# Three modulation sections of layer 0 moved from the Hyena and SSD stretch to the filters at the start

## The chip, the core and the metric

The kernel runs on one NeuronCore of a Trainium2 chip. Times are device microseconds of one launch. The engines are named as the profile names them: PE (TensorE matmul), PEld (its weight load), DVE (VectorE), ACT (ScalarE), POOL (GpSimd) and SP (SyncE, which here only issues DMAs).

## The reference

The program is two layers of a backbone for 512 latent tokens and 256 context tokens of width 1024, all in float32. A layer normalises the tokens, scales and shifts them by vectors that come from a conditioning vector, projects them with `w_in`, mixes them in four head groups (an SSD scan, a Hyena long convolution, windowed and dense attention), projects with `w_out`, gates and adds, and then does the same around a squared-ReLU MLP:

```python
mod = jax.nn.silu(c) @ w_mod[i] + b_mod[i]
sh1, sc1, g1, sh2, sc2, g2 = jnp.split(mod[:, None, :], 6, axis=-1)
h = rms_norm(x, norm_mix_pre[i]) * (1.0 + sc1) + sh1
y, yc = token_mixers(h, hc, ...)
x = x + g1 * rms_norm(y, norm_mix_post[i])
h = rms_norm(x, norm_mlp_pre[i]) * (1.0 + sc2) + sh2
x = x + g2 * rms_norm(squared_relu_mlp(h, mlp_w1[i], mlp_w2[i]), norm_mlp_post[i])
```

The six modulation vectors of a layer are six sections of 1024 columns of `w_mod`. Section 2 is the gate `g1` that follows `w_out`; sections 3 and 4 are the shift and scale ahead of the MLP; section 5 is the gate behind it. None of them depends on the tokens. The Hyena filters do not depend on the tokens either: for each layer and length a small network gives two-sided filters, which are multiplied by fixed decay factors, normalised and transformed to a spectrum.

## The kernel before

**The order of the work.** The program is written in one order, and a planner then orders the instructions of each engine by program order, by priority and by its own estimate of when each is ready. The order on each engine and on each DMA queue is fixed from then on. An instruction that waits holds up all that stands behind it on its engine or queue.

**The beginning** (to about 152 us) consists of these parts. `filter_head` makes the input of the filters. A first weave, to about 57 us, alternates sections 0 and 1 of layer 0 (`mod_cols`, tiles `wm`, six buffers, PSUM tile `pmod`) with the filters of layer 0 for 512 tokens (`filter_seq`, variant "0"). `pre` loads two token tiles, takes their norm and scales them; `pre_pair` transposes them on PE and splits each result into a high and a low part for the projections. `load_units(1, 0)` loads the first two units of `w_in`. Then come the filters of layer 1 for 512 tokens and those of layer 0 for 256, and `qkv_in` with the units dq and dkv (dense attention); the unit cq (windowed attention) follows in `layer`. Every projection is three matmuls for each product (`mm3`, lines 298 to 300).

**The ring `raw`.** A unit of weights is loaded in two halves of 512 KB. Each half goes into a tile `r` of the pool `raw`, which has three buffers, and is split by ACT (line 265) and DVE (line 270) into a tile `w` of the pool `wsp`, which has four. The three token pairs of `pre` use `wsp` too. Outside the first weave, `mod_section` loads its pieces of `w_mod` (512 KB each) into the same ring `raw`. `load_units` issues at high priority.

**A modulation section** in `mod_section` is eight steps. A step loads 128 rows of `w_mod` and multiplies them on PE with four float32 matmuls that write to four groups of PSUM partitions (line 449; the trace counts two records for each, so eight records a step). Then come four small copies by ACT (line 457). `mod_cols` adds eight tiny transposes (line 510) and one or two small DVE operations; `mod_gate` loads four rows on SP's queue (line 526), does four DVE operations (line 528) and writes two rows out on POOL's queue (line 530). In the MLP the sections are summed by DVE instead (`mod_sums`).

**The Hyena and SSD stretch** of a layer follows attention and the rest of the projections. In layer 0 it lies from about 395 to 543 us: `weave` alternates the Hyena operator for 512 tokens, that for 256, the SSD scan and, two steps at a time, four modulation sections: 2, 3 and 4 of layer 0 (`mod_list(0)[0:3]`) and section 0 of layer 1 (`mod_first(1)[:1]`). In layer 1 the same stretch has no modulation section.

**Decay factors.** `filter_seq` loads a tile `dec` (two buffers) from `decay` four times for each layer and length, once for each order and channel half, on SP's queue at high priority; each load waits until the DVE operation of line 679 that read the buffer before is done.

Of the kernel before, what the change touches and what calls it, by code (L numbers as in the profile page):

```python
# [22 lines left out]
SEQ = 512  # L23
CTX = 256
# [137 lines left out]
PRIO_W = 4000  # L162
# [3 lines left out]
ME = (4, 1, 2)  # L166
# [7 lines left out]
def chain(*gens):  # L174
    for g in gens:
        yield from g
# [7 lines left out]
class K:  # L184
# [420 lines left out]
    def filter_loads(self):  # L605
        self.mark("filters")
        nc, A = self.nc, self.A
        self.st = "f"
        pf = self.fpar = self.sm(4, F32, "pf")
        nc.sync.dma_start(pf, A["pf"])  # L610
        nc.vector.tensor_scalar(pf[:, 2:4], pf[:, 2:4], 1.0 / (2 * math.pi), None, MUL)
        zf = self.zf = self.a("fh")
        nc.sync.dma_start(zf[:HY_EMB], A["zfeat"])
        w12 = self.w12 = self.a("fw", (2, 128))
        nc.vector.memset(w12[:, 1], 0.0)
        nc.sync.dma_start(w12[:HY_EMB, 0], A["hw1"])
        for l in range(DEPTH):
            r = slice(64 * l, 64 * l + 64)
            nc.sync.dma_start(w12[r, 1, r], A["hy_w2"][l])
        self.w3 = self.a("fw3")  # L620
        nc.sync.dma_start(self.w3, A["hw3"])

    def filter_head(self):

# [31 lines left out]
    def filter_seq(self, l, n, tabs, v=""):  # L656
        self.mark("filter_seq")
        nc, A = self.nc, self.A
        self.st = "f"
        big = n == SEQ  # L660
        off = 0 if big else SEQ
        h = n // 2
        nj = 2 if big else 1
        nb = 2 * nj
        rl = slice(64 * l, 64 * l + 64)
        for o in range(2):
            ss = self.sm(4, F32, "ss")
            kds = []
            for c in range(2):
                kd = []  # L670
                dec = self.a("dec")[:, :n]
                with self.tc.high_priority(offset=PRIO_W):
                    nc.sync.dma_start(dec, A["decay"][c][:, off:off + n])
                for d in range(2):
                    p = self.a("pf1")[:, :n]
                    ch = 4 * o + 2 * d + c
                    nc.tensor.matmul(p, self.w3[rl, 128 * ch:128 * ch + 128], self.h2[rl, off:off + n], start=True, stop=True)
                    t = self.a("kd" + v)[:, :n]
                    nc.vector.scalar_tensor_tensor(t, p, self.pp[l][:, P_B3 + ch:P_B3 + ch + 1], dec, ADD, MUL)
                    nc.scalar.activation(p, t, AF.Square, accum_out=ss[:, 2 * d + c:2 * d + c + 1])  # L680
                    kd.append(t)
                    yield
                kds.append(kd)
            ms = self.sm(2, F32, "ms", 4)
            nc.vector.scalar_tensor_tensor(ms, ss[:, 0:2], EPS, ss[:, 2:4], ADD, ADD)
            r = self.rsqrt(ms, 2)
            yield
            for c in range(2):
                nc.vector.memset(kds[c][1][:, 0:1], 0.0)
                nc.scalar.activation(kds[c][1], kds[c][1], AF.Copy, scale=r[:, c:c + 1])  # L690
            for cs in range(2):
                X = [self.a("fx" + v, (nb, 256)) for _ in range(2)]
                for c in range(2):
                    kd = kds[c]
                    src = self.a("ko" + v)[:, :n]
                    nc.vector.scalar_tensor_tensor(src, kd[0], r[:, c:c + 1], kd[1], MUL, SUB if cs else ADD)
                    p = self.a("pf2")
                    for par in range(2):
                        for jc in range(nj):
                            s = src[:, 256 * jc + par:256 * jc + 256:2]  # L700
                            b = par * nj + jc
                            nc.tensor.transpose(p[:, 128 * b:128 * b + 128], s, self.ident)
                    pv = p[:, :128 * nb].rearrange("p (b c) -> p b c", c=128)
                    self.hi(X[0][:, :, 128 * c:128 * c + 128], pv)
                    self.lo(X[1][:, :, 128 * c:128 * c + 128], pv, X[0][:, :, 128 * c:128 * c + 128])
                    yield
                for kc in range(h // 128):
                    p = self.a("pmod" if not v and kc % 2 else "pf3")
                    for par in range(2):
                        for jc in range(nj):  # L710
                            b = par * nj + jc
                            if big:
                                th, tl = (tabs[2 * cs + par][:, jc, q, 128 * kc:128 * kc + 128] for q in range(2))
                            else:
                                th, tl = (tabs[0][:, cs, par, q, :] for q in range(2))
                            self.mm3(p[:, 256 * par:256 * par + 256], th, tl,
                                     X[0][:, b, :], X[1][:, b, :], jc == 0, jc == nj - 1)
                    od = self.t2((128, 256))
                    kt = self.a("fk" + v, (2, 256))
                    nc.scalar.activation(od, p[:, 256:512], AF.Copy)  # L720
                    nc.vector.tensor_tensor(kt[:, 0, :], p[:, 0:256], od, ADD)
                    nc.vector.tensor_tensor(kt[:, 1, :], p[:, 0:256], od, SUB)
                    for half in range(2):
                        dst = self.spec[l, n][kc + half * (h // 128)][:, 512 * cs + 256 * o:512 * cs + 256 * o + 256]
                        nc.gpsimd.dma_start(dst, kt[:, half, :])  # L725
                    yield
# [607 lines left out]
    def run(self):  # L1334
        nc = self.nc
        self.plan()
        self.setup()
        pf = self.push("fil", {"fh": (768, F32, 2), "fw": (256, F32, 1),
                               "kd": (512, F32, 4), "ko": (512, F32, 2),
                               "fk": (512, F32, 1), "fw3": (1024, F32, 1), "dec": (512, F32, 2),  # L1340
                               "ft": (1024, F32R, 4), "fx": (1024, F32R, 3)}, "right")
        pp = self.push("pp", {"pf1": (512, F32, 2), "pf2": (512, F32, 2), "pf3": (512, F32, 1),
                              "pmod": (512, F32, 1), "pg": (512, F32, 2)}, psum=True)
        fl = self.push("filL", {"kd0": (512, F32, 8), "ko0": (512, F32, 4), "fk0": (512, F32, 2), "fx0": (1024, F32R, 4), "wm": (1024, F32, 6)})
        self.filter_loads()
        tb = self.filter_tables(SEQ)
        self.filter_head()

        def pre(pair):
            self.mark("pre")  # L1350
            x2 = self.wsp_p.tile([128, 2, 4 * WU], F32, tag="w", name=self.nm("w"))
            xr2 = [x2[:, i, 0:1024] for i in range(2)]
            for i in range(2):
                nc.sync.dma_start(xr2[i], self.x_in(0, 2 * pair + i))
            self.pre_norm(xr2, xr2)
            return xr2
        xr = [pre(0)]
        self.weave((chain(self.mod_cols(0, 0, 0), self.mod_cols(0, 1, 1, P_NMIX)), W0[0]),
                   (self.filter_seq(0, SEQ, tb, "0"), W0[1]))
        self.pop(fl)  # L1360
        XTp = self.push_xt()
        fa = self.push("qkv", self.QKV_TAGS)
        XT = self.new_xt()
        xr += [pre(1), pre(2)]
        for pair in range(3):
            self.mark("pre")
            self.pre_pair(xr[pair], pair, XT, self.mods[0, 1], self.mods[0, 0], EN[0])
        self.load_units(1, 0)
        if self.nl > 1:
            self.do(self.filter_seq(1, SEQ, tb))  # L1370
        self.do(self.filter_seq(0, CTX, self.filter_tables(CTX)))
        self.setup2()
        self.qkv = self.qkv_in(0, "d", XT)
        self.pop(pp)
        self.pop(pf)
        for l in range(self.nl):
            XT, XTp, fa = self.layer(l, XT, XTp, fa)

    def layer(self, l, XT, XTp, fa):
        nc = self.nc  # L1380
        need = l < DEPTH - 1
        nt = NT if need else 4
        n = 128 * nt
        more = l + 1 < self.nl
# [27 lines left out]
        YT = self.new_xt((0,), need)  # L1412
        self.load_units(self.upos[l, "o", 3])
        hys = [(self.hyena(l, SEQ, 0, YT), W2[0])]
        mods = self.mod_list(l)[0 if l == 0 else ME[0]:3 if l == 0 and more else 9]
        if need:
            hys.append((self.hyena(l, CTX, SEQ, YT), W2[3]))
        if l + 1 < self.nl:
# [215 lines left out]
```

## Time and profile before

| | |
|---|---|
| median of 3 timed runs | 1924.27 us (1921.92 to 1924.78) |
| time of the profiled execution | 1919.0 us |
| its span, first to last instruction | 1917.2 us |
| mean granted clock of TensorE | 0.974 |
| busy in the span: PE, PEld, DVE, ACT, POOL | 93%, 77%, 68%, 44%, 5% |
| DMA over the span | 235.16 MB, mean 123 GB/s |

The span is that of the profiled execution, 1.8 us shorter than its time. Busy PE time is modelled from pipelined matmuls, so that a stretch can be full of matmuls and still wait in places. Shares over the whole span are means over stages with different limits.

### The profile page before, as it was taken

The numbers are of one execution on the slowest core, as the hardware profiler recorded it, in microseconds if no ns is written. First come the engines' busy times: TensorE is split into PE (matmuls) and PEld (weight loads), VectorE is DVE, ScalarE is ACT, GpSimd is POOL, SyncE is SP. The second block draws the span as 40 slices with busy tenths as digits, with TensorE's granted clock in tenths as the row PEclk, the third lists the DMA queues.
The fourth block names the chain that finished last, engine by engine and source line by source line (L and its number), as shares of the span: only waits on it lengthen the run. The fifth ranks groups of instructions, "written<-read, shape, count | busy, mean of one in ns | idle before, by whom it ended". The sixth has DMA issues, their size and how long they took to land.

```text
span 1917.2 us, 27370 instructions
## 1 busy us (share of the span) xinstructions
PE 1790.2 (93%) x10170; PEld 1482.7 (77%) x10170; DVE 1297.7 (68%) x2897; ACT 836.8 (44%) x1804; POOL 91.5 (5%) x176
## 2 busy tenths in 40 slices
PE   6899999978879999999999998899978789999998
PEld 2688888845668888888888888888866688888886
DVE  4878888877756656676666658988878563444446
ACT  4844565536515532322222327556546263332322
POOL 0120001011000000000000000000010000000000
PEclk9999999989989999999999999999989899999999
DMA  8531121278833244333333415112183243233232
GB/s 291 187 111 53 39 74 58 69 260 272 290 107 132 93 135 136 121 107 114 121 121 121 142 47 176 45 48 89 45 273 120 74 157 113 91 99 99 88 102 85
DMA packets 137597, 235.16 MB, mean 123 GB/s; under 512 B 12466, under 2 KB 77395, under 8 KB 137464
## 3 DMA queue, kind: packets, MB, share of 16 engines
q1 hardware_dynamic: 122920, 186.12, 30.2%
q0 software_dynamic: 14544, 47.30, 7.1%
q8 instruction: 80, 1.31, 0.3%
q14 instruction: 53, 0.43, 0.1%
HBM read 206.74 MB, written 26.64 MB: 122 GB/s over the span
## 4 chain that ended last, share of the span: by engine, by line
PE 76%; DVE 9%; issue 6%; DMA 4%; ACT 4%; POOL 1%; SPq 0%; DVEq 0%; ACTq 0%; POOLq 0%
PE pg L298 19%; PE pg L299 18%; PE pg L300 18%; PE po L1294 3%; PE py L298 2%; PE py L299 2%; PE pm L1286 2%; PE py L300 2%; PE ps L1249 1%; PE ps L1250 1%; PE pm L1206 1%; PE psd L1052 1%; DMA spec<-fk 1%; POOL spec L725 1%; DMA r<-in_w_mod_dram 1%
## 5 line engine op out<-in xcount | busy, mean ns | idle before, releaser
L265 ACT ACTIVATE w<-r 128x1024 fp32r<-128x1024 f32 (+1 forms) x176 | 186.6, 1061 | 348.1 <-PE pg L300 325.1
L270 DVE TENSOR_TENSOR w<-r,w 128x1024 fp32r<-128x1024 f32 (+1 forms) x176 | 214.1, 1223 | 106.1 <-ACT w L265 105.2
L298 PE MATMUL pg<-xl,w 128*128 128x512 f32 (+1 forms) x704 | 269.5, 386 | 2.2 <-DVE ya L1311 0.9
L300 PE MATMUL pg<-xl,w 128*128 128x512 f32 (+1 forms) x704 | 269.7, 384 | 0.0
L299 PE MATMUL pg<-xl,w 128*128 128x512 f32 (+1 forms) x704 | 269.7, 384 | 0.0
L298 PE MATMUL pg<-w,H 128*128 128x512 f32 x640 | 250.1, 391 | 0.0
L299 PE MATMUL pg<-w,H 128*128 128x512 f32 x640 | 249.2, 390 | 0.0
L300 PE MATMUL pg<-w,H 128*128 128x512 f32 x640 | 249.0, 389 | 0.0
L476 DVE SCALAR_TENSOR_TENSOR x<-r,scT,x 128x512 f32<-128x512 f32 x168 | 119.1, 746 | 71.7 <-DMA r<-in_w_mod_dram 71.7
L298 PEld LDWEIGHTS pg<-xl,w 128*128 128x128 f32 x704 | 132.6, 190 | 27.7 <-issue 2.2
L300 PEld LDWEIGHTS pg<-xl,w 128*128 128x128 f32 x704 | 133.3, 189 | 22.9
L299 PEld LDWEIGHTS pg<-xl,w 128*128 128x128 f32 x704 | 133.3, 189 | 22.2 <-DVE xl L270 0.2
L298 PEld LDWEIGHTS pg<-w,H 128*128 128x128 f32 x640 | 120.1, 188 | 26.8 <-issue 1.7
L300 PEld LDWEIGHTS pg<-w,H 128*128 128x128 f32 x640 | 120.1, 188 | 25.0
L299 PEld LDWEIGHTS pg<-w,H 128*128 128x128 f32 x640 | 120.2, 188 | 24.4
L1520 ACT ACTIVATE t<-pg 128x512 f32<-128x512 f32 (+1 forms) x100 | 50.4, 506 | 198.0 <-PE pg L300 198.0
L1551 DVE TENSOR_TENSOR ya<-pg,ya 128x512 f32<-128x512 f32 x120 | 81.8, 687 | 69.0 <-PE pg L300 68.7
L1522 DVE TENSOR_TENSOR t<-t 128x512 f32<-128x512 f32 (+1 forms) x100 | 58.1, 582 | 83.7 <-ACT H L1521 83.6
L300 PE MATMUL pg<-xc,w 128*128 128x256 f32 (+1 forms) x368 | 104.4, 284 | 0.0
L298 PE MATMUL pg<-xc,w 128*128 128x256 f32 (+1 forms) x368 | 103.3, 284 | 1.1 <-ACT xc L265 1.1
L299 PE MATMUL pg<-xc,w 128*128 128x256 f32 (+1 forms) x368 | 104.1, 284 | 0.0
L298 PE MATMUL pg<-w,xl 128*128 128x256 f32 (+1 forms) x320 | 93.0, 292 | 5.4 <-ACT qk L1113 2.5
(357 smaller groups left out, 3866.1 us busy)
## 6 DMA issues: line engine op xcount, KB each, us to landing
r<-in_mlp_w_dram SPq DMA_DIRECT2D x128, 512.0 KB
r<-in_w_mod_dram SPq DMA_DIRECT2D x80, 512.0 KB
r<-in_w_in_dram SPq DMA_DIRECT2D x40, 512.0 KB
ht<-in_inv_dram POOLq DMA_DIRECT2D x20, 512.0 KB, 5.4
ht<-in_fwd_dram POOLq DMA_DIRECT2D x18, 512.0 KB, 5.4
wm<-in_w_mod_dram SPq DMA_DIRECT2D x16, 512.0 KB
r<-in_w_out_dram SPq DMA_DIRECT2D x16, 512.0 KB
xd<-x POOLq DMA_DIRECT2D x16, 512.0 KB, 3.3
```

Source lines behind the costliest of these rows:

```text
L265: self.nc.scalar.activation(dst, src, AF.Copy)
L270: self.nc.vector.tensor_tensor(dst, src, h.bitcast(F32), SUB)
L298: mm(out, ah, bh, start=first, stop=False)
L299: mm(out, ah, bl, start=False, stop=False)
L300: mm(out, al, bh, start=False, stop=last)
L476: nc.vector.scalar_tensor_tensor(acc[:, c], raw[:, k], sc, acc[:, c], MUL, ADD)
L725: nc.gpsimd.dma_start(dst, kt[:, half, :])
L1286: nc.tensor.transpose(p[:, n:n + 128], P[:, col:col + 128], self.ident)
L1294: nc.tensor.matmul(po[:, qo:qo + m], V[:, c, :], pt[:, hl, cols[j]:cols[j] + m], start=i + j == 0 and hl == 0, stop=i + j == len(kts) - 1 ...
L1520: nc.scalar.activation(r, p[:, :nn], AF.Relu)
L1522: nc.vector.tensor_tensor(r, r, r, MUL)
L1551: nc.vector.tensor_tensor(dst, p, dst, ADD)
```

## The change

Sections 2, 3 and 4 of layer 0 are no longer in the Hyena and SSD stretch. A new function `filters_rest` runs the filters of layer 1 for 512 tokens and those of layer 0 for 256, and a weave alternates two steps of it with one step of the three sections; the stretch keeps section 0 of layer 1 alone. Section 5 stays in the MLP. The tile `pmod` is now in use by the sections while these filters run, so every second transform in `filter_seq` takes a buffer of `pf2` instead. `decays` loads the two decay tiles once for 512 tokens (in `filter_loads`, in front of everything in the first weave) and once for 256, at ordinary priority. The slice of `mods` in `layer` is now empty for layer 0; for layer 1 it is empty before and after.

```diff
@@ -619,6 +619,14 @@
             nc.sync.dma_start(w12[r, 1, r], A["hy_w2"][l])
         self.w3 = self.a("fw3")
         nc.sync.dma_start(self.w3, A["hw3"])
+        self.decays(SEQ)
+
+    def decays(self, n):
+
+        off = 0 if n == SEQ else SEQ
+        self.dec = [self.a("dec")[:, :n] for _ in range(2)]
+        for c in range(2):
+            self.nc.sync.dma_start(self.dec[c], self.A["decay"][c][:, off:off + n])
 
     def filter_head(self):
 
@@ -668,9 +676,7 @@
             kds = []
             for c in range(2):
                 kd = []
-                dec = self.a("dec")[:, :n]
-                with self.tc.high_priority(offset=PRIO_W):
-                    nc.sync.dma_start(dec, A["decay"][c][:, off:off + n])
+                dec = self.dec[c]
                 for d in range(2):
                     p = self.a("pf1")[:, :n]
                     ch = 4 * o + 2 * d + c
@@ -705,7 +711,7 @@
                     self.lo(X[1][:, :, 128 * c:128 * c + 128], pv, X[0][:, :, 128 * c:128 * c + 128])
                     yield
                 for kc in range(h // 128):
-                    p = self.a("pmod" if not v and kc % 2 else "pf3")
+                    p = self.a("pf2" if not v and kc % 2 else "pf3")
                     for par in range(2):
                         for jc in range(nj):
                             b = par * nj + jc
@@ -1366,15 +1372,19 @@
             self.mark("pre")
             self.pre_pair(xr[pair], pair, XT, self.mods[0, 1], self.mods[0, 0], EN[0])
         self.load_units(1, 0)
-        if self.nl > 1:
-            self.do(self.filter_seq(1, SEQ, tb))
-        self.do(self.filter_seq(0, CTX, self.filter_tables(CTX)))
+        self.weave((self.filters_rest(tb), 2), (chain(*self.mod_list(0)[:3 if self.nl > 1 else 4]), 1))
         self.setup2()
         self.qkv = self.qkv_in(0, "d", XT)
         self.pop(pp)
         self.pop(pf)
         for l in range(self.nl):
             XT, XTp, fa = self.layer(l, XT, XTp, fa)
+
+    def filters_rest(self, tb):
+        if self.nl > 1:
+            yield from self.filter_seq(1, SEQ, tb)
+        self.decays(CTX)
+        yield from self.filter_seq(0, CTX, self.filter_tables(CTX))
 
     def layer(self, l, XT, XTp, fa):
         nc = self.nc
@@ -1412,7 +1422,7 @@
         YT = self.new_xt((0,), need)
         self.load_units(self.upos[l, "o", 3])
         hys = [(self.hyena(l, SEQ, 0, YT), W2[0])]
-        mods = self.mod_list(l)[0 if l == 0 else ME[0]:3 if l == 0 and more else 9]
+        mods = [] if l == 0 else self.mod_list(l)[ME[0]:]
         if need:
             hys.append((self.hyena(l, CTX, SEQ, YT), W2[3]))
         if l + 1 < self.nl:
```

## Rows read from the trace of the kernel before

**Rows 1.** Busy time by stage: core 0, the columns named in the first line
```profile
core 0: us, PE busy (x) PEld busy (x) DVE busy (x) ACT busy (x) POOL busy (x), PEclk, DMA share, GB/s
...
20.00:57.00 37.00, 35.51 (x240) 16.07 (x239) 25.89 (x82) 20.83 (x48) 2.17 (x4) 1.00 0.77 272
57.00:91.00 34.00, 26.28 (x157) 19.02 (x156) 29.38 (x104) 30.58 (x62) 6.45 (x12) 1.00 0.53 175
91.00:152.00 61.00, 58.19 (x436) 54.41 (x434) 43.62 (x136) 30.39 (x84) 13.45 (x25) 0.97 0.33 102
152.00:390.00 238.00, 231.56 (x1562) 204.19 (x1561) 202.87 (x541) 135.67 (x356) 15.90 (x29) 0.99 0.19 59
...
430.00:530.00 100.00, 89.82 (x655) 61.35 (x652) 69.69 (x173) 57.75 (x185) 9.23 (x18) 0.93 0.82 278
1440.00:1480.00 40.00, 34.41 (x216) 25.77 (x217) 34.63 (x87) 27.63 (x92) 2.14 (x5) 1.00 0.32 103
```

**Rows 2.** Chain that ended last, 430 to 545 us, by line
```profile
by line: DMA r<-in_w_mod_dram 9.4%; PE pg L449 8.8%; DMA hf<-spec 8.7%; PE psd L1052 8.5%; DMA t<-us 4.4%; PE psd L1043 4.2%; DMA gated<-t 3.8%; issue 3.4%; PE ph L298 3.3%; PE ps L1063 3.1%; DVE wx L270 3.0%; PE ph L300 2.7%; PE ph L299 2.
```

**Rows 3.** Busy time of line L449 alone: PE, PEld, clock, DMA share, GB/s
```profile
430.00:530.00 100.00, 20.29 (x208) 3.90 (x208) 0.93 0.82 278
```

**Rows 4.** Timeline of SP's queue in the beginning: start, duration, what
```profile
12.38 3.07 SPq L447 DMA_DIRECT2D wm<-in_w_mod_dram  x6
...
38.86 2.78 SPq L447 DMA_DIRECT2D wm<-in_w_mod_dram  x5
49.19 0.33 SPq L673 DMA_DIRECT2D dec<-in_decay_dram  x1
49.57 0.90 SPq L1354 DMA_DIRECT2D w<-in_x_dram  x2
...
59.30 0.33 SPq L673 DMA_DIRECT2D dec<-in_decay_dram  x1
59.67 1.53 SPq L354 DMA_DIRECT2D r<-in_w_in_dram  x3
```

**Rows 5.** Waits of SP's queue, 0 to 180 us: total, times, longest
```profile
SPq L673 <- DVE kd L679: 48.0, 7, 11.9
```

**Rows 6.** Timeline of DVE: the splits of w_in halves that free raw
```profile
78.88 1.23 DVE L270 TENSOR_TENSOR w<-r,w 128x1024 fp32r<-128x1024 f32 x1 [0.25 <-ACT w L265]
...
90.55 1.22 DVE L270 TENSOR_TENSOR w<-r,w 128x1024 fp32r<-128x1024 f32 x1
...
93.84 1.22 DVE L270 TENSOR_TENSOR w<-r,w 128x1024 fp32r<-128x1024 f32 x1
```

**Rows 7.** Timeline of SP's queue in layer 0's MLP
```profile
656.13 2.76 SPq L354 DMA_DIRECT2D r<-in_mlp_w_dram  x2
661.17 8.12 SPq L469 DMA_DIRECT2D r<-in_w_mod_dram  x2
```

**Rows 8.** Timeline of PE: first matmul of dq and of cq
```profile
91.61 0.39 PE L298 MATMUL pg<-w,xl 128*128 128x256 f32 x1 [0.26 <-ACT t L598]
...
153.28 0.39 PE L298 MATMUL pg<-w,xl 128*128 128x256 f32 x1 [1.11 <-DVE V L270]
```

**Rows 9.** Chain that ended last, first weave: one step, one group of transposes
```profile
31.53 0.54 PE pmod L449 x8
...
38.11 0.67 PE pmod L510 x8
```

**Rows 10.** Groups by line, 395 to 545 us: busy, mean ns, idle before
```profile
L457 ACT ACTIVATE t<-pg 2x256 f32<-2x256 f32 x16 | 5.9, 372 | 0.2
...
L528 DVE TENSOR_TENSOR t<-t,t 2x512 f32<-2x512 f32 x4 | 2.6, 672 | 0.0
```

**Rows 11.** Line L449 over the whole run: waits for DMA, us and times
```profile
  DMA r<-in_w_mod_dram: 8.6, 8
```

**Rows 12.** Timeline of SP's queue: first and last w_mod load from 395 us
```profile
397.58 0.33 SPq L447 DMA_DIRECT2D r<-in_w_mod_dram  x1
...
504.58 1.41 SPq L447 DMA_DIRECT2D r<-in_w_mod_dram  x2
```

## The prediction

> **What bounds the kernel now.** I read the profile by stage first, because the page's shares are means over stages that have different limits. The reader is to see three regimes in [rows 1]. From 91 to 390 us PE is full: 58.19 of 61 us, then 231.56 of 238. What is added to PE there moves everything behind it, and there DMA is at 0.33 and 0.19 of its engines. From 430 to 530 us, the middle of layer 0's Hyena and SSD stretch, DMA is at 0.82, PE at 90% and DVE at 70%: no engine is full, and waits between them set the pace. From 57 to 91 us PE is idle for 34 − 26.28 = 7.7 us, while ACT and DVE are at 90% and 86%.
>
> Next I read the chain that ended last, because it says which waits of the stretch count [rows 2]. In its 115 us from 430 to 545, waiting for pieces of `w_mod` is 9.4% (10.8 us), the matmuls of line 449 are 8.8% (10.1 us), and the write of the gate rows to memory 3.8% (4.4 us). Then come loads that are not the sections' own but run beside them: 8.7% for spectra (10.0 us) and 4.4% for `us` (5.1 us). Line 449 alone is 20.29 us of PE from 430 to 530 [rows 3].
>
> Last I read SP's queue at the beginning, because two things change there. Loads of `dec` wait on the DVE work of line 679 for 48.0 us in seven waits [rows 5]. What they hold up: the queue has nothing to do from 41.64 us (38.86 + 2.78) until the decay load at 49.19, and the next token tiles follow right behind it; again until 59.30, and the first `w_in` halves follow at 59.67 [rows 4].
>
> **The change, part by part.**
>
> *Matmuls in the beginning, +14.3 us.* Three sections are 24 steps. A step on the chain is 0.54 us, and a group of transposes 0.67 us [rows 9]; two sections have transposes. 24 × 0.54 + 2 × 0.67 = 14.3 us. Where do they fall? A piece of `w_mod` needs a buffer of `raw`, and the ring follows program order: in the MLP two unit halves and then two pieces take turns although the units have the higher priority [rows 7]. So the pieces come behind the four halves of dq and dkv. The first buffer comes free at 78.88 + 1.23 = 80.1 us, the others at 91.8 and 95.1 [rows 6], and dq starts at 91.61 [rows 8]. The sections therefore run beside dq and dkv, where PE is full, and only the first piece or two reach the idle time ahead of 91 us. I count all 14.3 us. Their twelve copies on ACT (12 × 0.372 = 4.5 us) and four DVE operations (4 × 0.672 = 2.7 us [rows 10]) lie beside a PE that is full, in a stage where ACT is at 50% and DVE at 72% [rows 1]: nothing.
>
> *Waits for the pieces, +3 us.* PE is in order, so a step whose piece is late stops dq too. Line 449 waits 8.6 us for DMA over its 48 steps [rows 11]. If all of that belongs to the 32 steps that use `raw`, 24 steps cost 6.5 us; the bound below is 0, because DMA is at 0.33 there and not at 0.82. I take 3, about the middle.
>
> *Decay loads, −5 us.* Twelve loads become four. The two for 512 tokens wait for nothing. Without the waits the token tiles can be issued some 8 us earlier (41.64 in place of 49.57) and `w_in` as well, so ACT can take their norms while it has room and dq starts earlier. The gain is bounded by PE's idle time from 57 to 91 us, 7.7 us, and by 0 below, if DVE at 86% holds the rest back. I take 5, nearer the upper end because ACT, the fuller of the two, is the one relieved. The two loads for 256 tokens wait for the last use of the old factors in layer 1's filters; behind them on SP's queue stand pieces of `w_mod` (counted under the pace below).
>
> *Other edits, 0.* Four transforms take a buffer of `pf2`, which also holds the transposes; dq and dkv cover the wait. If that cover were gone, four waits of about one DVE split (1.23 us [rows 6]) would cost 5 us. The gate's four rows on SP's queue, and its two writes on POOL's queue with the spectra behind them, delay the filters, not dq or dkv; the filters are next needed in the Hyena stretch.
>
> *The stretch, −22 us.* All steps behind the first eight go, 24 of 32; the first eight (layer 1's section 0) take the place of section 2 in its start. So nothing changes until about 430 us, and nearly all of [rows 3] goes. Two ways to the size. By the chain: 10.8 + 10.1 + 4.4 = 25.3 us belong to the moved sections, and 40 us if the loads beside them also become free (10.0 + 5.1 more). By density: layer 1's stretch without sections holds DVE and PE at 34.63 and 34.41 of 40 us (87% and 86%) in its middle. What is left in layer 0's 100 us is PE 89.82 − 20.29 × 24/26 = 71.1 and DVE 69.69 − 2.6 = 67.1; at those densities it takes 83 and 78 us, a gain of 17 to 22. I take 22, where the two nearly meet. The bounds are 10.8 us (only the waits for the pieces go) and 40.
>
> *Sum:* 14.3 + 3 − 5 − 22 = −9.7. The profiled execution took 1919.0 us (span 1917.2 and 1.8 around it), so 1909.3. The median of the runs is 5.3 us above the profiled one; with that, 1914.
>
> **The rivals.**
>
> *Only the waits go, chance 0.17.* In the stretch PE was not full, so its 10.1 us of line 449 may turn into waits for something else. Then the gain is 10.8 + 4.4 = 15.2 us, and the sum −2.9: 1921, no change that shows. For it speaks that DVE and the SSD scan alternate there with PE; against it that line 449 stands on the chain. The Trainium skill ("Perfetto Trace Analysis", Identifying the Most-Contended Engine) tells to judge TensorE by its weight-load share and to relieve the most contended engine first; by that the change loads the full stage and relieves PE where it was not the limit. The trace agrees on the shares: PEld is 54.41 of 61 us from 91 us on, and 61.35 of 100 in the stretch [rows 1].
>
> *The ring holds back `w_in`, slower, chance 0.22.* The halves of cq now stand behind all 24 pieces. Before, cq started at 153.28 us [rows 8]; with the terms above it is due at 153.3 + 14.3 + 3 − 5 = 165.6. Its first half takes the buffer of piece 22. The ring runs at full rate from about 90 us (95.1 − 5); with p us a piece, 6 us for two section borders and 7 us for landing and split (estimates from the copies, transposes, and split above and a load's wait in the stretch), cq is ready at 103 + 19p. Each us late is lost, since PE has nothing else. It is late from p = 3.3, and the gain is gone at p = 3.8. The trace has 16 pieces in 29.3 us with six buffers, 1.8 each [rows 4], and 31 in 108.4 us in the stretch, 3.5 each [rows 12]. I expect about 2.4, as DMA has room (0.33). At 4.3 cq is 19 us late and the kernel 9 us slower: 1933.
>
> *The beginning takes it nearly free, chance 0.16.* dq starts the full 7.7 us earlier, no piece is late, and the stretch gives all 25.3 us: 14.3 − 7.7 − 25.3 = −19, so 1906. ACT's and DVE's shares there speak against it.
>
> **How the numbers follow.** The forecast has 0.45, and what is a few us to either side of it is still faster. About 0.2% (3.8 us) is what can be told from no change. Faster: 0.45 less a little, 0.16 and a third of the first rival: 0.64. Same: the rest of that rival, 0.13. Slower: 0.23. The likeliest case's own range is 1907 to 1920. The range for all reaches down past the third rival, since the bound of the stretch (40) lies further, and up to the second: 1897 to 1932.
>
> **What would show each step.** Right: 24 steps of line 449 between about 75 and 150 us, at 0.54 us on the chain; dq's first matmul some 5 us ahead of 91.6; DMA at two thirds or more there; the stretch near 125 us from 395 in place of 148, without waits for `w_mod` behind 435. Wrong: PE idle ahead of cq with its split as releaser (second rival); PE waiting for `w_mod` for more than 6.5 us in the beginning; dq still at 91 us; a stretch shorter by less than 15 us, with the idle time on PE put down to DVE or ACT.

## The result, and the profile after

The changed kernel is slower by 0.9%: 1940.84 us (median of four runs, 1936.7 to 1941.5) against 1923.1 us beside it, a ratio of 1.0088 with a 95% interval of 1.007 to 1.0105. The forecast was 1914 us, in a range of 1897 to 1932.

Where the time went is read from the first instruction of each stage in the two profiled executions (spans 1917.2 and 1939.6 us; these two lie 22.4 us apart, the medians 17.7). dq's first matmul marks the end of what lies ahead of the projections, the first load of `hz` the start of the Hyena and SSD stretch, and the first matmul of `w_out` its end.

| stage | before | after | difference | the prediction's terms |
|---|---|---|---|---|
| to dq's first matmul | 91.6 | 91.4 | −0.2 | −5 |
| dq to the stretch | 301.4 | 331.7 | +30.3 | +14.3 + 3 |
| the stretch | 150.4 | 145.0 | −5.5 | −22 |
| behind it | 1373.7 | 1371.5 | −2.2 | 0 |

Three terms failed: dq comes no earlier, the move costs nearly twice as much between dq and the stretch, and it gives back a quarter in the stretch. Busy time by stage after, to be held against [rows 1]; the last row is the stretch as a whole, which begins 30 us later now:

```profile
core 0: us, PE busy (x) PEld busy (x) DVE busy (x) ACT busy (x) POOL busy (x), PEclk, DMA share, GB/s
57.00:91.00 34.00, 25.80 (x154) 19.68 (x152) 27.21 (x101) 29.25 (x57) 6.42 (x12) 0.95 0.27 91
91.00:152.00 61.00, 55.32 (x402) 36.73 (x400) 35.92 (x112) 21.87 (x61) 11.27 (x21) 0.89 0.71 224
152.00:180.00 28.00, 27.83 (x228) 23.11 (x226) 11.54 (x30) 10.97 (x33) 3.21 (x6) 1.00 0.64 195
...
423.13:568.10 144.97, 99.94 (x615) 75.73 (x614) 107.81 (x257) 69.97 (x205) 13.96 (x27) 0.85 0.63 193
```

From 91 to 152 us DMA has risen from 0.33 to 0.71, as the prediction wanted, but PE has lost 3 us of busy time, DVE 8, and the granted clock is 0.89. In the stretch PE is busy 99.94 us of 145, against 117.35 of 150.45 before:

```profile
393.05:543.50 150.45, 117.35 (x823) 79.15 (x823) 108.43 (x259) 73.17 (x216) 15.06 (x29) 0.86 0.79 264
```

Most of the 20.29 us of line 449 [rows 3] is gone, and the time hardly moved. PE was not what bound it.

The same for the blocks of dq and dkv, from dq's first matmul to dkv's last, before and then after:

```profile
91.61:152.20 60.59, 58.01 (x432) 54.29 (x432) 43.20 (x136) 29.79 (x82) 13.45 (x25) 0.97 0.33 103
```
```profile
91.40:182.50 91.10, 85.51 (x644) 62.34 (x645) 48.10 (x146) 34.28 (x95) 14.48 (x27) 0.93 0.68 210
```

The whole 30.5 us lie here. PE is busy 27.5 us longer: line 449 alone is 20.07 us, line 510 1.33, and the other matmuls take 27.5 − 21.4 = 6.1 us more (four small transposes of the filters among them, which lay ahead of dq before). Idle time is 3.0 us more (5.6 against 2.6). What stops the engines is in the waits from 91 to 185 us (engine, line, releaser; total, times, longest) and in the list of DMA issues from 91 to 165 us (the last number is the median us to landing):

```profile
POOL spec L731 <- DVE fk L727: 67.3, 11, 18.6
ACT t L726 <- PE pf L300: 22.2, 10, 6.5
DVE fk L727 <- DMA spec<-fk: 18.7, 7, 5.0
```
```profile
r<-in_w_mod_dram SPq DMA_DIRECT2D x24, 512.0 KB, 4.4
spec<-fk POOLq DMA_DIRECT2D x22, 128.0 KB, 4.6
```

The filters write each result into one buffer, `fk`, and POOL stores it to `spec`, the spectra in memory. Before, such a store landed in 2.1 us and DVE waited for one three times, 3.6 us in all:

```profile
DVE fk L721 <- DMA spec<-fk: 3.6, 3, 2.7
```

Beside the pieces of `w_mod` it lands in 4.6 us, and DVE waits 18.7 us. DVE works in its fixed order, so the projections' and filters' other work stands behind. One such wait on DVE's timeline, and PE's beside it, which is for a piece:

```profile
101.09 0.69 DVE L270 TENSOR_TENSOR fx<-pf,fx 128x512 fp32r<-128x512 f32 x1 [1.09 <-ACT fx L265]
105.50 0.42 DVE L727 TENSOR_TENSOR fk<-pf,t 128x256 f32<-128x256 f32 x1 [3.72 <-DMA spec<-fk]
```
```profile
102.64 0.61 PE L449 MATMUL pmod<-r,scT 128*2 128x256 f32 x8 [1.73 <-DMA r<-in_w_mod_dram]
105.42 1.03 PE L449 MATMUL pmod<-r,scT 128*2 128x256 f32 x8
```
```profile
99.00:103.00 4.00, 2.27 (x26) 1.37 (x18) 1.69 (x3) 1.81 (x5) 0.00 (x0) 1.00 0.85 269
103.00:107.00 4.00, 4.00 (x26) 1.97 (x19) 1.42 (x10) 0.00 (x0) 0.78 (x2) 0.62 0.71 240
107.00:111.00 4.00, 4.00 (x23) 2.92 (x23) 1.32 (x9) 1.60 (x3) 0.29 (x1) 0.53 0.77 215
```

PE idles 1.73 us at 101 us, and the granted clock is 0.62 and 0.53 for the eight us behind it. 1.00 is the level of 2.4 GHz, 0.5 that of 1.2, and the step at 105.42 takes 1.03 us where the one at 102.64 took 0.61. A wait (1.87 us, this time for DVE's line 728, which writes `fk`) and a fall come again at 141 us. Part of the slower matmuls comes from there: by the rows of the two blocks the lower level takes 0.07 × 91.1 = 6.4 us after and 0.03 × 60.6 = 1.8 us before, an estimate in which the steps have their share. Not every wait of PE is followed by a fall: from 115 to 119 us PE idles 1.4 us, and the clock stays at 1.00 until 145 us.

The Trainium skill has a line that bears on the stores ("Trainium Kernel Development and Optimization", Key Constraints): DMAs issued from SP, ACT and POOL run on the same 16 DMA engines and interleave. The trace agrees: POOL's stores went from 2.1 to 4.6 us beside SP's loads.

SP's queue shows the ring:

```profile
78.81 0.33 SPq L629 DMA_DIRECT2D dec<-in_decay_dram  x1
91.65 22.86 SPq L447 DMA_DIRECT2D r<-in_w_mod_dram  x10
...
124.89 33.90 SPq L447 DMA_DIRECT2D r<-in_w_mod_dram  x12
160.42 3.98 SPq L354 DMA_DIRECT2D r<-in_w_in_dram  x3
```

The first piece goes out at 91.65 us, when the split of a half of `w_in` frees a buffer, the last at 158.8: 67.1 us for 23 steps, 2.9 us a piece. The load of cq stands behind them, at 160.42. Its split is done at 170.0, but dkv keeps PE until 182.5.

### The profile page after: what moved, and what is told of

It reads as the page before. It is cut to its first block, busy times and chain, and to the rows that moved or that the text cites. A ratio compares the mean times of both kernels' runs of the same rounds, so it can differ in the third digit from the quotient of the medians.

```text
span 1939.6 us, 27349 instructions
## 1 busy us (share of the span) xinstructions
PE 1804.0 (93%) x10170; PEld 1486.8 (77%) x10170; DVE 1297.4 (67%) x2897; ACT 836.5 (43%) x1804; POOL 91.3 (5%) x176
## 3 DMA queue, kind: packets, MB, share of 16 engines
q1 hardware_dynamic: 121768, 184.28, 30.3%
## 4 chain that ended last, share of the span: by engine, by line
PE 77%; DVE 8%; issue 7%; DMA 4%; ACT 4%; POOL 1%; SPq 0%; DVEq 0%; ACTq 0%; POOLq 0%
PE pg L298 19%; PE pg L299 19%; PE pg L300 18%; PE po L1300 3%; PE py L298 2%; PE pm L1292 2%; PE py L299 2%; PE py L300 2%; PE ps L1255 1%; DMA ht<-in_inv_dram 1%; DMA spec<-fk 1%; PE ps L1256 1%; PE pmod L449 1%; PE pm L1212 1%; PE pf L683 1%
## 5 line engine op out<-in xcount | busy, mean ns | idle before, releaser
L299 PEld LDWEIGHTS pg<-w,H 128*128 128x128 f32 x640 | 120.2, 188 | 24.3
```

The lines of the kernel that those rows point to most:

```text
L299: mm(out, ah, bl, start=False, stop=False)
```

## The experiments

All are read by stage, from one trace each, because the start differs between executions (last section). A is the time from ACT's first split of `w_in` to the first load of the stretch. The timed ratio is against the kernel before on the same chip.

| kernel | ratio, 95% | A, us | stretch, us |
|---|---|---|---|
| before | | 328.3 | 150.4 |
| changed | 1.0088 (1.007 to 1.0105) | 359.9 | 145.0 |
| decay factors once alone | 1.0034 (1.001 to 1.0057) | 332.6 | 153.3 |
| the same, loaded first | 1.003 (1.0014 to 1.0046) | 333.5 | 152.5 |
| move alone | 1.0113 (1.0095 to 1.0131) | 360.4 | 144.4 |
| sections in both places | 1.0176 (1.0138 to 1.0214) | 355.0 | 155.6 |
| sections nowhere | 0.998 (0.9951 to 1.0008) | 335.1 | 145.6 |
| loads alone in the beginning | 1.0058 (1.0029 to 1.0087) | 345.4 | 146.0 |
| matmuls alone in the beginning | 1.0031 (1.0005 to 1.0057) | 338.6 | 145.4 |
| changed, second spec buffer | 1.0096 (1.0063 to 1.0128) | 354.9 | 145.9 |
| before, second spec buffer | 0.9987 (0.9972 to 1.0001) | 326.6 | 155.6 |
| changed, pieces in tiles of V | 1.0144 (1.0108 to 1.0181) | 365.6 | 142.8 |
| changed, sections after dq and dkv | 1.0236 (1.0211 to 1.0261) | 381.6 | 144.3 |
| before, four table buffers | 1.0039 (1.0025 to 1.0053) | 329.1 | 161.6 |
| before, SSD first | 1.0015 (1.0004 to 1.0027) | 330.0 | 150.4 |
| changed, SSD first | 1.008 (1.0052 to 1.0108) | 358.3 | 126.7 |
| move, SSD first | 1.0056 (1.004 to 1.0072) | 358.2 | 128.2 |
| move, SSD first, second spec buffer | 0.9999 (0.9983 to 1.0014) | 349.5 | 125.2 |

**The two halves of the change.** First the decay factors without the move, then the move without them:

```diff
-        self.weave((self.filters_rest(tb), 2), (chain(*self.mod_list(0)[:3 if self.nl > 1 else 4]), 1))
+        self.do(self.filters_rest(tb))
...
-        mods = [] if l == 0 else self.mod_list(l)[ME[0]:]
+        mods = self.mod_list(l)[0 if l == 0 else ME[0]:3 if l == 0 and more else 9]
```

> The decay factors loaded once and the bank of PSUM exchanged, with the three sections left in the Hyena and SSD stretch as before. If the sections are what costs (main theory): within 5 us of the kernel before, 1919 to 1926 us, the stretch still about 150 us, dq's first matmul still near 91 us because ACT's scaling of the transposes (L598) stands behind the filter's own ACT work. If loading the decay factors once is what costs (rival: the first load of the context's factors holds SP from 79 to 92 us): 1928 to 1941 us.

```diff
...
-                dec = self.dec[c]
+                dec = self.a("dec")[:, :n]
+                with self.tc.high_priority(offset=PRIO_W):
+                    nc.sync.dma_start(dec, A["decay"][c][:, off:off + n])
...
```

> The three sections moved to the beginning, the decay factors loaded for every filter as before. Main theory (sections cost, decay factors are neutral): 1936 to 1944 us, as the changed kernel. Rival (decay factors cost): 1915 to 1928 us.

The loss belongs to the move: 1942.6 us with it alone. The decay factors (with the transforms in `pf2`, which stayed) are no gain but a small loss, 1925.7, and dq began at 101.8 us in that profile, not near 91 as expected; its runs spread from 1920 to 1936 us, and the profiled one, 1934.4, is among the slow ones. Beside the move they are no loss: 1.0088 with them, 1.0113 without.

**The sections in both places, and in none.**

```diff
-        mods = [] if l == 0 else self.mod_list(l)[ME[0]:]
+        mods = self.mod_list(l)[0 if l == 0 else ME[0]:3 if l == 0 and more else 9]
```

> The three sections computed in the beginning and once more in the stretch. Main theory: the beginning is 30 us longer by itself and the stretch is back at its 150 us, so 1923 + 30 = 1953, less what the beginning's steps of before's stretch do not cover: 1943 to 1955 us, and the first load of the Hyena stretch at about 423 us. Theory of the prediction (the stretch gains its 22 us and something else behind it is lost): the stretch about 125 + 22 us, 1960 us or more.

```diff
-        self.weave((self.filters_rest(tb), 2), (chain(*self.mod_list(0)[:3 if self.nl > 1 else 4]), 1))
+        self.do(self.filters_rest(tb))
+        self.mods[0, 2], self.mods[0, 3] = self.mods[0, 0], self.mods[0, 1]
+        self.gates[0, 2] = self.tc.dram_tile([2, 1024], F32, name="gated_fake")
+        nc.gpsimd.dma_start(self.gates[0, 2], self.A["w_mod"][0, 0:2, 0:1024])
```

> The three sections left out in both places: layer 0's MLP takes the shift and scale of the mixer, and its gate for w_out is two rows copied from w_mod. This prices the stretch without the beginning. Main theory (the sections only filled gaps of a chain of waits in the stretch): the stretch 145 us instead of 150, the time 1914 to 1920 us. Theory of the prediction (their loads and steps were worth 22 us there): 1897 to 1904 us.

Both prices stand by themselves. Twice: dq to the stretch is 327.6 us, nearly as in the changed kernel, and the stretch 155.6 us; the time, 1956.05, is just above what was expected. Nowhere: the stretch is 145.6 us with no section in the beginning, and the kernel is within 0.2% of before (0.5% below the one with the decay factors alone, which it has too). So the stretch, as it is ordered, is worth 5 to 10 us, and even a free beginning would have given hardly anything.

**Loads or steps?** The beginning with one of the two, the stretch without sections as in the run before. The generators that take the sections' place:

```diff
...
+                raw = self.raw_p.tile([128, 1024], F32, tag="r", name=self.nm("r"))
+                self.nc.sync.dma_start(raw, self.A["w_mod"][0, 128 * k:128 * k + 128, 1024 * s:1024 * s + 1024])
...
```

> In the beginning only the 24 loads of w_mod, woven and placed in the ring as in the changed kernel, no matmul and no transpose on them; nothing of the three sections in the stretch (layer 0's MLP takes the mixer's shift and scale, and its gate is two rows copied from w_mod). Measured from dq's first matmul to the first load of the Hyena stretch: 301 us before, 305 with the decay factors alone, 307 with the sections nowhere, 332 in the changed kernel. Theory contention (the pieces slow the filter's spec stores, DVE waits for their buffer and all behind it waits too): 315 to 322, the spec stores at 4 us or more. Rival, the steps alone: 304 to 309, stores near 2 us. Rival, the ring: cq's split waits for its load, with PE idle ahead of it, 318 or more.

```diff
...
+                for q in range(4):
+                    self.nc.tensor.matmul(p[32 * q:32 * q + 2, 0:256], self.scT[:, k, :],
+                                          self.w3[:, 256 * q:256 * q + 256], start=k == 0, stop=k == 7)
...
```

> In the beginning only the matmuls and copies of the 24 steps, on a tile that lies in SBUF already (the filter's third weight), without the loads; nothing of the three sections in the stretch, as in the kernel with the loads alone. From dq's first matmul to the first load of the stretch: theory contention, 14.3 us of steps on a full PE above 304 to 307, so 318 to 322. Rival, the steps cost the whole 25 to 30 us (each slower than in the row, or the clock falls through them): 329 to 336. Rival, free: 304 to 309.

From dq to the stretch the loads alone give 317.1 us (within the first theory's 315 to 322), spec stores at 4.7 us, 20.2 us of DVE's waits for them, a clock of 0.84 from 91 to 152 us, with no step of a section there; with the steps alone the stores land in 2.1 us as before. So it is the loads that slow the stores. The steps alone give 308.7, in the range of "free" and not 318: with no piece to wait for they begin at 65.5 us, and 64 of their 192 records fall ahead of dq (102.2 in that trace), where PE has room. The other 128 take 9.58 us of PE, 0.60 a step, and yet the stage is only 1.7 us longer than with the sections nowhere (307.0), for PE's idle time in it falls from 11.8 us to 7.1: the steps fill waits. Against that same run A is 10.3 us longer with the loads, 3.5 with the steps, 24.8 with both. The loads are the dearer half, and 11 us come only together. The traces show where they lie: in the changed kernel PE idles 11.8 us from dq to the stretch, as with the sections nowhere, but all 24 steps fall behind dq, at 0.84 us each.

**A second buffer for the spec stores**, in the changed kernel and as a control in the kernel before:

```diff
-                    kt = self.a("fk" + v, (2, 256))
+                    if not v and not hasattr(self, "fk2"):
+                        self.fk2 = self.a("fh")[:, :512].rearrange("p (a b) -> p a b", a=2)
+                    self.tog = not getattr(self, "tog", False)
+                    if not v and self.tog:
+                        kt = self.fk2
+                    else:
+                        kt = self.a("fk" + v, (2, 256))
```

> The changed kernel with a second buffer for the filters' results that wait for their spec store (half of a buffer of the filter's head that is free by then). Theory contention: DVE no longer waits for a store (18.7 us before), and dq's first matmul to the stretch falls from 332 to 318 to 326; 1928 to 1936 us. Rivals (steps alone, ring): unchanged within 3 us, 1938 to 1943.

> The kernel before, nothing moved, with the second buffer for the filters' results that wait for their spec store. It is the control for the 10 us that this buffer gave where the sections stand beside the filters. Theory (it pays only because the pieces of w_mod slow the spec stores from 2.1 to 4.6 us): within 3 us of the kernel before, 1918 to 1924 us, from w_in's first split to the stretch 325 to 330 us. Rival (one buffer was too few in any case): 1908 to 1914 us and 316 to 320.

DVE has no wait for a spec store left among its longer ones, though the stores are no faster (4.8 and 5.5 us for the two buffers). The stage that had a clock of 0.89 reads, in the changed kernel with the second buffer:

```profile
91.00:152.00 61.00, 53.09 (x421) 37.21 (x423) 42.69 (x129) 31.30 (x78) 11.25 (x21) 1.00 0.66 215
```

From dq on the stage takes 324.5 us, inside 318 to 326, but A fell by 5.0 us only, and the time did not follow: 1939.09 us, in the rivals' 1938 to 1943. In this trace dq began at 102.0 us; it is the slowest of four runs (1933.9 to 1945.6), and where dq began in the others is not known, so the start may hide the gain here. The pair at the end of the table, which loads the decay factors as the kernel before does, tells it better: 1931.89 us without the buffer, 1921.28 with it, 10.6 us, and a clock from 91 to 152 us of 0.89 without and 1.00 with it. In both pairs PE waits longer for pieces with the buffer (5.1 us against 2.0, 4.4 against 1.1) and the clock doesn't fall in this stage, so it is DVE's waits, and not PE's for the pieces, that the falls go with. In the kernel before the buffer makes no difference that is clear of noise (0.1%): it pays under the pieces' traffic.

**Other places for the pieces.** First own buffers, the tiles `V`, which the projections write only later; then the sections written after the first projections:

```diff
...
+            for k0, kn, q0, qn in [(k, 1, 0, 3) for k in range(8)] + [(0, 3, 3, 1), (3, 3, 3, 1), (6, 2, 3, 1)]:
+                raw = self.a("V", (kn, 256 * qn)).bitcast(F32)
...
```

> The changed kernel with the pieces of w_mod in the four tiles that V will use, which are free until the projections write them, in 11 loads a section (eight of 384 KB and three of the rest) instead of the ring that they shared with w_in. Theory: in the ring the first piece waits until 91.65 us for a buffer that w_in's split frees, so all steps fall where PE is full and the spec stores are slowed; in own buffers they start near 55 to 65 us, as the matmuls without loads did (65.5), and the time from w_in's first split to the stretch falls from 360 to 342 to 350 us; 1924 to 1934 us. Rival, the ring doesn't matter, only the traffic: 354 to 362 us and 1936 to 1943.

```diff
...
         self.qkv = self.qkv_in(0, "d", XT)
+        self.do(chain(*self.mod_list(0)[:3]))
```

> The three sections neither woven with the filters nor in the stretch, but written after the first projections, so that their pieces load when the filters' spec stores are done; decay factors once. Theory (of the 27 us that the move costs, about 15 are steps on a full PE and the rest is the pieces' traffic against the spec stores and the fall of the clock behind it): from w_in's first split to the stretch 344 to 352 us (360 in the changed kernel, 333 with the decay factors alone), DVE's waits for spec stores under 6 us in all, stretch 145: 1928 to 1936 us. Rival (the steps cost the whole 27 us wherever PE is full): 356 to 362 us, 1938 to 1943.

Both miss. In V's tiles the first piece goes out at 78.92 us and not before, because a load of the decay factors for 256 tokens stands ahead of it on SP's queue and waits until 78.49; and ACT's writes to V then wait 12.5 us for the steps that read them. The stores are slowed less there (3.1 us, and 8.1 us of DVE's waits), which doesn't outweigh it. Written late, the steps come back to back with nothing woven between, wait for their loads (with their weight loads 50.5 us), and the clock is 0.50 from 180 to 215 us. Neither tells anything of the ring; the second shows what the steps cost with no other work between them.

**What sets the stretch?** First suspect: the Hyena's tables, which its chain waits for.

```diff
...
-                               "sf": (512, F32, SF[0] if need else SF[2]), "sy": (256, F32, 3 if need else 6), "sz": (256, F32, 4)}, "right")
-        hyt = {"hz": (512, F32, 2), "hf": (512, F32, SF[1] if need else SF[3]), "ht": (1024, F32R, 3 if need else 6), "hx": (1024, F32R, 2),
+                               "sf": (512, F32, 4 if need else SF[2]), "sy": (256, F32, 3 if need else 6), "sz": (256, F32, 4)}, "right")
+        hyt = {"hz": (512, F32, 2), "hf": (512, F32, 5 if need else SF[3]), "ht": (1024, F32R, 4 if need else 6), "hx": (1024, F32R, 2),
...
```

> The kernel before, sections in the stretch, with four buffers for the tables of the Hyena transforms instead of three, paid with one buffer each of the Hyena's and the SSD's temporaries (6 to 5, 5 to 4). Theory: the stretch is a chain through the loads of these tables, into which the steps of the sections fall as filling; a fourth buffer shortens it from 150 to 140 to 146 us, 1913 to 1919 us. Rival, the chain of DVE and ACT sets it: no shorter than 149 us.

It became longer, 161.6 us; so that theory had nothing for it (the two temporaries that paid for the buffer, `sf` and `hf`, may be what was lost). Then each half alone, in one execution each, `self.ssd(l, YT)` or `*hys` taken out of layer 0's weave:

> The sections nowhere, as in the run before it, and layer 0's SSD left out of the stretch (its four channels of the mixer's output are set to zero). Hyena alone. If the Hyena chain (transform tables and dependent work on DVE and ACT) sets the stretch: 125 to 145 us instead of 145.6. If the SSD sets it: 70 to 110 us.

> The sections nowhere, and layer 0's two Hyenas left out of the stretch (their channels are set to zero). SSD alone. If the Hyena chain sets the stretch: 50 to 90 us. If the SSD sets it: 120 us or more.

```profile
397.87:485.70 87.83, 57.89 (x381) 46.25 (x380) 64.31 (x143) 19.10 (x35) 13.87 (x26) 0.83 0.87 286
```
```profile
392.40:519.10 126.70, 73.36 (x341) 45.73 (x341) 67.87 (x172) 61.61 (x188) 2.70 (x5) 0.68 0.31 101
```

Hyena alone takes 87.8 us; the SSD alone 126.7, with PE at 58%, DVE 54%, ACT 49%, DMA 0.31 (it has no `hz` load; the window begins two us ahead of its first load, as in the others). No engine is full: it is a chain, and its waits name one another:

```profile
DVE sf L1053 <- ACT sf L1051: 22.6, 11, 4.5
PEld psd L1049 <- ACT sf L1047: 13.2, 7, 2.9
ACT sf L1051 <- PE psd L1049: 12.6, 12, 1.8
```

In the changed kernel this chain ends last, 14 us behind the Hyena's last transform, and PE waits for its normalised tokens at the end of the stretch:

```profile
PE psd L1089 <- DVE sz L1084: 12.7, 1, 12.7
```

So the SSD was put first in the weave, with two steps a turn:

```diff
-        self.weave(*hys, (self.ssd(l, YT), W2[1]), (chain(*mods), W2[2]))
+        self.weave((self.ssd(l, YT), 2), *hys, (chain(*mods), W2[2]))
```

> The kernel before with the SSD first in the weave of the stretch and two of its steps a turn, in both layers; sections in the stretch. Hyena alone takes 88 us there, the SSD alone about 125, both with the sections 150. Theory (the SSD's chain of dependent work is the longest, and what stands between its steps lengthens it): the stretch 130 to 145 us and 1905 to 1918 us. Rival (the three strands share DVE, so that the order doesn't matter): 148 to 154 us, 1919 to 1926.

> The same order of the weave in the changed kernel. Theory (the SSD's chain): the stretch 128 to 140 us instead of 145, and the sections' move still costs 25 to 30 us ahead of it: 1925 to 1936 us. Rival: 143 to 148 us, 1937 to 1943.

In the kernel before nothing moves, 150.4 us: the SSD's last matmul comes 140 us into the stretch instead of 147, but the Hyena's last transform 142 instead of 139. In the changed kernel the stretch falls from 145.0 to 126.7 us, as long as the SSD alone:

```profile
421.83:548.50 126.67, 94.91 (x616) 70.96 (x614) 100.98 (x244) 68.76 (x203) 13.89 (x27) 0.89 0.67 208
```

The equal length doesn't prove that the SSD's chain is all that is left: alone it ran at a clock of 0.68, here at 0.89. The time, 1937.92 us, is in the rival's range; its runs spread from 1928 to 1944 us, which may be the start, and layer 1 had changed too. So the last two keep the first loads and layer 1's order as before, with and without the second spec buffer:

> The three sections moved as in the changed kernel, decay factors loaded for every filter as before, the second buffer for the spec stores, and in layer 0's stretch the SSD first with two steps a turn (layer 1's order as before). Theory (the move's 22 us lie in the stretch, hidden by the SSD's late order; its price ahead is some 20 us with the second buffer): the stretch 126 to 132 us, from w_in's first split to the stretch 348 to 356 us, 1912 to 1922 us. Rival (what the order gave belongs to the start of TensorE or to layer 1): 1930 to 1940 us.

> The same without the second buffer for the spec stores. Theory: the stretch 126 to 132 us, from w_in's first split to the stretch 355 to 361 us, 1917 to 1926 us: no clear difference from the kernel before, as the stretch gives back what the beginning costs. Rival: 1930 to 1940 us.

1931.89 us against 1942.64 for the move alone (1.0056 against 1.0113): the order is worth about 11 us. Both stages came out as expected, and the time did not: it missed 1917 to 1926 and lies in the rival's 1930 to 1940, for the stretch is 16.2 us shorter, and 5.3 come back right behind it (from its end to the end of the kernel 1377.6 us against 1372.3; why is not known). With the second buffer 1921.28, no different from the kernel before, and the lower end of what was expected wasn't reached. No version here beats the kernel before.

## Why the prediction was wrong, by its steps

*Matmuls in the beginning, +14.3.* They fell where the prediction put them, beside dq and dkv on a full PE (first piece at 91.65 us). But the size was off: 21.4 us, 0.84 us a step instead of 0.54, since part ran at the lower clock level (1.03 us a step) and part was cut up by other matmuls; and the matmuls beside them took 6.1 us more, in part through the clock. The sum had the clock at nothing.

*Waits for the pieces, +3.* PE's idle time grew by just 3.0 us, 2.0 of it in two waits for pieces; that the sizes agree is in part luck. The step that failed is what stood around this term: the prediction asked who waits for the pieces, and not whom the pieces make wait. It counted only the 8.6 us of [rows 11]. It even named the POOL queue with the spectra and dismissed it ("delay the filters, not dq or dkv"). The loads alone, without a step, lengthened this stage by some 10 us: DVE waited 20.2 us for the stores of the one buffer `fk`, and the clock was 0.84. Together with the steps nearly all of the price shows as PE's busy time (27.5 of 30.5 us), since the steps fill the waits.

*Decay loads, −5.* The tiles came earlier (42.15 us instead of 49.57) and dq did not. ACT's scaling of the transposes (line 598) began at 77.2 us, against 75.0 before, in its place behind the filters' work on ACT. TensorE began earlier too, at its lower level (last section).

*Other edits, 0.* Decay factors and transforms together cost 0.3%. Which of the two it is was not taken apart: the four waits for `pf2` that the prediction priced at 5 us without cover would be of that size, and with the decay factors alone PE waits 3.2 us in three for the DVE line that empties a transform's buffer (728; 722 before), against 0.6 in one before.

*The stretch, −22.* Measured −5.5, the step that failed furthest. Both ways to its size, the chain and the density, took what stood on the path away and assumed nothing right behind. The SSD's chain stood there; woven last, it lets the stretch end only 5 us earlier without the sections. The 22 us did exist: with the SSD first the stretch is 126.7, 23.7 us below the kernel before. In the kernel before the same order gives nothing; the sections' loads still fill DMA there (0.80 from 430 to 530 us), but that they are the reason is not shown. Neither edit alone reaches it.

*The rivals.* "Only the waits go" came nearest for the stretch: busy time of line 449 turned into waits for something else. The page of the Trainium skill quoted there, judged against the result, was right that PE was not the limit that the change relieved. The ring did hold `w_in` back, with 2.9 us a piece (between the 1.8 of [rows 4] and the 3.5 of [rows 12]) and cq's load at 160.42 us, but PE still had dkv for 12.5 us after cq's split; it cost nothing. (The rival's formula, 103 + 19p, gives 158 us for the end of that split; it came at 170.0.) The third never came near. Of the signs set down, DMA at two thirds came true; "a stretch shorter by less than 15 us" and "dq still at 91" named the failures. The forecast's last addition was rounded down: 1909.3 and 5.3 are 1914.6.

## What to carry to other kernels

Before loads are moved to where DMA has room, look for small stores there whose single buffer an engine waits for, with other work behind it; give it a second buffer first. The Trainium skill ("Perfetto Trace Analysis", Optimization Strategy) says that a gap that repeats can mean too few buffers. The trace agrees: the seven waits of DVE's line 727 for a store, 18.7 us, went with a second buffer. And when work is taken off a chain of waits, ask for the next longest chain by running it alone: the gain ends there, unless the order lets that chain start first.

## What the runs showed of the hardware

TensorE's start differs with what is loaded first, and between executions with one order of loads, and dq moves by up to 12 us. In the twelve traces in which the decay loads stand behind the filters' weights, the first matmul comes at 7.9 to 8.9 us, and the first 4 to 11 steps of `w_mod` take 1.03 us each; the first whole step at 0.61 comes at 33 to 34 us in seven of them and at 51 to 60 in five, and dq begins at 90 to 93 us in the seven and at 99 to 102 in the five. Ahead of that time PE had been busy nearly without a gap from about 17 us. The rows print a granted clock of 1.00 there, but only because the trace holds no record of the clock yet: the first record, of the higher level, lies at 30.7 to 32.5 us in the seven and at 50.6 to 56.6 in the five, at most four us ahead of the first whole step at 0.61.

With these loads in front (eight traces), the first matmul comes at 12 to 14 us and the first record at 21.2 to 24.4, in one at 35.3. Steps that come ahead of it are slow there too; in the kernel before, whose first record lies at 23.8 us, they are two, in one row:

```profile
22.10 1.86 PE L449 MATMUL pmod<-wm,scT 128*2 128x256 f32 x16
```

So TensorE's first steps are slow in the kernel before too; what goes with the order is how early the clock rises.

The run to test the order had the factors loaded once, but first (the kernel before, one of the three traces that its text counts as free of slow steps, has those of the row above):

> The decay factors once, as in the run with them alone, but their loads at high priority, so that the first two stand first on SP's queue as in the kernel before; sections in the stretch as before. Seven traces with the loads behind the filter's weights have TensorE's first matmul at 8 to 9 us and then 4 to 9 steps of w_mod at 1.03 us before the steps take 0.61; the three traces with the loads first have it at 12 to 14 us and none at 1.03. Theory (it is the order of these loads that starts TensorE so): no step at 1.03, dq's first matmul at 89 to 94 us, 1915 to 1922 us. Rival (fewer loads, not their order): 4 or more steps at 1.03, dq at 90 to 102, 1920 to 1936.

The start was as in the kernel before, with the first record at 24.3 us and steps at 0.61 from 25.2. But the granted clock fell later, and steps took 1.03 us again:

```profile
24.00:36.00 12.00, 11.98 (x70) 3.65 (x70) 7.08 (x26) 6.80 (x16) 0.00 (x0) 1.00 0.83 278
36.00:48.00 12.00, 11.41 (x54) 3.94 (x54) 7.16 (x19) 5.31 (x13) 0.00 (x0) 0.58 0.79 286
```

dq began at 98.1 us, and the time was 1927.87: in the end the rival's numbers fit, not the theory's. What decides how long TensorE stays at the lower level at the start, and why one order of loads gives two starts, stays open.
